# Last pair of heads: splits of the output weights held behind scaled k, the projection's shares in another order, and the second feed-forward's first weights laid off the residual

## The chip, the cores and the metric

The kernel runs on one core of one Trainium2 chip. The metric is the device time of one execution in microseconds (us). Before the change it was 1968.99 us, the median of three runs (1968.15 to 1970.13).

## What is computed

One layer of a macaron block on x of 1024 rows by 1024 columns, in float32: a half-weighted SwiGLU feed-forward (inner width 2816), stick-breaking attention with 16 heads of 64, and a second half-weighted SwiGLU feed-forward. Each part has an RMS norm in front of it and is added to the residual x.

```
x = x + 0.5 * swiglu(rms_norm(x, n1), wi1, wo1)
xn = rms_norm(x, mix_norm)
q, k, v = heads(xn @ w_qkv);  q, k = rms_norm(q, q_gain), rms_norm(k, k_gain)
z = q @ k^T / 8
w[t, s] = sigmoid(z[t, s]) * prod over s < j < t of (1 - sigmoid(z[t, j])),  for s < t
x = x + concat_heads(w @ v) @ w_o
x = x + 0.5 * swiglu(rms_norm(x, n2), wi2, wo2)
```

## The kernel before

**Numbers in two parts.** A matmul operand is kept as a high part (`fp32r`, written by ACT in `split`, L179) and a low part (operand minus high part, written by POOL or DVE, L180). `mm3` (L271 to L273) multiplies high by high, low by high and high by low, three matmuls for each step of the contraction.

**Stages.** The first feed-forward and the second one work by seven half-size products each. Between them stand the attention and its output projection. The rows t lie in two halves of 512, each in blocks `tb` of 128; `ORDER` names the blocks as 4, 5, 6, 7, 0, 1, 2, 3.

**Attention.** The heads are taken in eight pairs p. One pair has four parts a, b, c, d (`PARTS`, 61 units of time together), one for each head and half of the rows. Every step of the attention is put into `plan` with a time in these units, and the steps are recorded in the order of their times (L970): the scores of a block (`scores`, L817 to L830: matmul, two sigmoids on ACT, a scan on DVE, a product on POOL), the turn of the weights on PE and their split (`turn`, L852), the product with v (`apply`, L870), the q, k, v of the next pair (`qkv`), and the scaled and turned q and k (`prep_q`, `prep_k`, L775 to L780). At the end of q, k, v of a half, POOL writes scaled k into `qk` (L755, L758). Each engine works off its own list in order, so a step that waits holds up what stands behind it on that engine.

**Output of a pair.** For pairs 0 to 6 the result o is split and stored to the scratch tensors `o_keeph` and `o_keepl` (L884) by SP's DMA queue; `load_o` (L895) reads them back into `xh` and `xl`, half 1 of the rows in the seventh pair and half 0 in the eighth. The eighth pair's o is split straight into `xh` and `xl` (L886).

**Projection.** w_o is taken in two halves of its columns. For the first half `out_weights` (L984) loads two k-blocks at a time into `raw0` or `raw1` in turn (512 KB, L987) and splits them; there are four such loads, wo0 to wo3, and the third and fourth reuse the buffers of the first and second. `ON_POOL` says whose low part goes to POOL (all four; DVE's otherwise), `WO_FIRST` into which tiles the parts go. `project(tb, ks, 0)` adds the product of row block tb over the pairs ks to the residual half `x0` (DVE, L1000). `SHARES` gives the times within the last pair at which the eight blocks get their sum over k = 0 to 6, so that this work fills PE beside the last pair's attention; the eight products with k = 7, which need the last pair's o, follow after it. Then come the second half's weights and products (k = 0 to 7, into `x1`), with the norm of finished blocks beside them.

**Places in memory.** The pools of `PROJECTION` lie in one stretch of SBUF in the order of the list, and the second feed-forward's tiles are laid over the same stretch later: a tile of the later stage waits for the last reader of what lay there. `first_weights` (L335) splits the first eight units of w2_in into the tiles u0 to u7, before the stream of further weights begins; `first_pair` (L344) multiplies with them: for the first 256 columns of rows all four products, and in front of the fourth `turn_rest`, the last transposes of the normed rows.

**What sets the order.** Every instruction gets a rank when it is recorded; what is recorded `as_at(mark)` gets the rank of that mark. A scheduler then fills each engine's list by rank and by when its own model has the operands ready, so work of a late rank can be moved ahead into a gap of the model. The marks of the shares come from the plan; w_o's first loads and splits have `marks[0]` (d 15.5 of the seventh pair), and stand earlier than that in the lists.

Of the kernel before, what the change touches and what calls it, by code (L numbers as in the profile page):

```python
# [9 lines left out]
F32 = mybir.dt.float32  # L10
# [3 lines left out]
ALU = mybir.AluOpType  # L14
# [3 lines left out]
P = 128  # L18
# [8 lines left out]
NP = H // 2  # L27
# [3 lines left out]
ORDER = (4, 5, 6, 7, 0, 1, 2, 3)  # L31

BANKS = {"bz": 3, "bq": 2, "bt": 2, "bo": 1, "ka": 2, "kc": 2, "kb": 4, "ma": 4, "mb": 4}

ON_POOL = {"wo0", "wo1", "wo2", "wo3"}

# [6 lines left out]

LOADS = (("c", 14.0), ("c", 15.0), ("d", 9.0), ("d", 10.0))

SHARES = (("b", 6.0), ("b", 11.0), ("c", 3.0), ("c", 9.0), ("c", 15.0), ("d", 1.5), ("d", 5.0), ("d", 8.5))

TURN, APPLY = 4.0, 2.3  # L50
RAW = 6
# [2 lines left out]
U_TILES = 18  # L54
# [35 lines left out]
    6: ((0, 1), (0, 0), "subtract"), 7: ((1, 0), (1, 1), "subtract"),  # L90
}

SHARE = 7


PROJECTION = ("wa", "x0", "wb", "wc", "we", "wf", "wg", "wd", "wh", "wi", "wj", "wk", "wl", "x1")
WO_FIRST = ("raw2", "raw3", "raw4", "raw5", "wa", "wb", "wd", "wc")
WO_SECOND = ("we", "wf", "wg", "wh", "wi", "wj", "wk", "wl")
EARLY = ("bq",)
ROUND = ("bq", "bt", "bq", "bt", "bo")  # L100
# [3 lines left out]
def macaron_kernel(ctx, tc, x, g1, w1_in, w1_out, gm, w_qkv, gq, gk, w_o, g2, w2_in, w2_out, out):  # L104
# [8 lines left out]
    def lane(name):  # L113

        return pool_e if name in ON_POOL else dve

# [52 lines left out]
    make_identity(nc, ident)  # L169
    xh = cpool.tile([P, KD, T], F32R, name="xh")  # L170
    xl = cpool.tile([P, KD, T], F32R, name="xl")
    above = cpool.tile([P, 112], F32, name="above")
    pool_e.memset(below, 0.0)
    pool_e.memset(above, 0.0)
    x_keep = [dram.tile([T, D], F32, name=f"x_keep{i}") for i in range(2)]
# [2 lines left out]
    def split(raw, hi, lo, engine=None):  # L178
        act.activation(hi, raw, AF.Copy)  # L179
        (engine or dve).tensor_tensor(lo, raw, hi.bitcast(F32), op=ALU.subtract)  # L180
# [151 lines left out]

    T0, T1 = HALVES[1], HALVES[0]

    def first_weights(pl, raws, behind=None):  # L335

        place["u"] = place["h"] = 0
        return {
            (j, part): [unit(pl, columns(raws[part][d], j), pool_e, behind) for d in range(2)]
            for part in range(2)  # L340
            for j in range(2)
        }

    def first_pair(pl, us, turns):  # L344

        hb = {}
        n = 0  # L350
        for t, c in ((0, T0), (1, T1)):
            ps = {key: bank("ka" if key[1] == 0 else "kc") for key in us}
            for c0 in range(0, NHALF, CHUNK):
                cc = slice(c.start + c0, c.start + c0 + CHUNK)
                for i, (key, w) in enumerate(us.items()):
                    if (n, i) in turns:
                        turns[n, i]()
                    mm3(
                        ps[key][:, c0 : c0 + CHUNK],
                        [  # L360
                            ((w[k // 4][0][:, k % 4], w[k // 4][1][:, k % 4]), (xh[:, k, cc], xl[:, k, cc]))
                            for k in range(KD)
                        ],
                    )
                n += 1
            for j in range(2):
                h = small(pl, "h")
                g = pl[f"h{place['h'] + 3}"].tile([P, NHALF], F32, name="h", bufs=1)
                act.activation(g, ps[j, 0], AF.Silu)
                dve.tensor_tensor(h, ps[j, 1], g, op=ALU.mult)  # L370
                hb[j, t] = h
        return hb
# [299 lines left out]
    on_banks = ExitStack()  # L672
    on_banks.enter_context(banks("psa"))

    marks = []
    with ExitStack() as stack:
        pl = dict(stack.enter_context(pools(
# [247 lines left out]
        for p in range(-1, NP):  # L925
            this = states[p] if p >= 0 else None
            nxt = states[p + 1] if p < NP - 1 else None
            start, t = {}, PAIR * p
            for part, span in PARTS.items():
                start[part], t = t, t + span  # L930

            def put(part, t, f):
                plan.append((start[part] + t, f))

            for part, span in PARTS.items():
                state = nxt if part == "d" else this
                if state is not None:
                    spread(scores(state, *UNITS[part]), start[part], start[part] + span, 0.5)
                if this is not None:
                    groups = values(this, p, *BEFORE[part])  # L940
                    for i, (to_turn, to_apply) in enumerate(groups):
                        t = TURN + (span - TURN) * i / len(groups)
                        put(part, t, to_turn)
                        put(part, t + APPLY, to_apply)
            if nxt is not None:
                if p >= 0:
                    fills = qkv(p + 1, nxt)
                    for part, span in PARTS.items():
                        for i in range(FILLS[part]):
                            put(part, (span - (3.0 if part == "d" else 0.0)) * (i + 0.5) / FILLS[part], fills.pop(0))  # L950
                put("c", 15.0, partial(prep_q, nxt, 1))
                put("c", 17.5 if p >= 0 else 20.0, partial(prep_k, nxt, 0, 1))
                put("d", 8.0, partial(prep_k, nxt, 1, 1))
            if this is not None:
                put("a", 5.0, partial(prep_q, this, 0))
                put("a", 7.5, partial(prep_k, this, 0, 0))
                put("b", 8.0, partial(prep_k, this, 1, 0))
            if 0 <= p < NP - 2:

                held = (lambda s=nxt: s["qk", 1][:, 0, 4, 0:1], lambda s=nxt: s["qk", 0][:, 2, 0, 0:1])  # L960
                for at, f in zip(LOADS, weights_of(p + 2, states[p + 2], held)):
                    put(*at, f)
            if p == NP - 2:
                put("c", 10.0, partial(load_o, 1))
                put("d", 15.5, lambda: marks.append(tc.cur_priority))
            if p == NP - 1:
                put("a", 2.5, partial(load_o, 0))
                for at in SHARES:
                    put(*at, lambda: marks.append(tc.cur_priority))
        for _, f in sorted(plan, key=lambda e: e[0]):  # L970
            f()
# [8 lines left out]
    with pools(*PROJECTION) as pl:  # L980
        pl = pl | pr | pn
        x_sb = [pl[f"x{h}"].tile([P, NT, NHALF], F32, name=f"x{h}", bufs=1) for h in range(2)]

        def out_weights(c, k, rooms):  # L984

            raw = pl[f"raw{k // 2 % 2}"].tile([P, D], F32, name="raw", bufs=1)
            sp.dma_start(  # L987
                raw.rearrange("p (k c) -> p k c", k=2),
                w_o[k * P : (k + 2) * P, c].rearrange("(k p) c -> p k c", p=P),
            )  # L990
            h_, l_ = (pl[n].tile([P, D], F32R, name=n.rstrip("2345"), bufs=1) for n in rooms[k : k + 2])
            split(raw, h_, l_, lane(f"wo{k // 2}") if c is HALVES[0] else dve)
            return [(h_[:, s], l_[:, s]) for s in HALVES]

        def project(tb, ks, h, tags):

            o = any_bank(tags)
            t = rows(tb)
            mm3(o, [((xh[:, k, t], xl[:, k, t]), wo[k]) for k in ks])
            dve.tensor_tensor(x_sb[h][:, tb, :], o, x_sb[h][:, tb, :], op=ALU.add)  # L1000

        wo = []
        place["raw"] = 2
        for k in range(0, NP, 2):
            with as_at(marks[0]):
                wo += out_weights(HALVES[0], k, WO_FIRST)
        with as_at(marks[0]):
            for tb in ORDER:
                sp.dma_start(x_sb[0][:, tb, :], x_keep[0][rows(tb), HALVES[0]])
        for i, tb in enumerate(ORDER):  # L1010
            with as_at(marks[1 + i]):
                project(tb, range(SHARE), 0, EARLY)
        for tb in ORDER:
            sp.dma_start(x_sb[1][:, tb, :], x_keep[0][rows(tb), HALVES[1]])
        gain = load_gain(pl, g2)
        for tb in ORDER:
            project(tb, range(SHARE, NP), 0, ROUND)
        wo = []
        for k in range(0, NP, 2):
            wo += out_weights(HALVES[1], k, WO_SECOND)  # L1020
        ahead = [stream(pr, w2_in, 0, part) for part in range(2)]
        for i, tb in enumerate(ORDER):
            project(tb, range(NP), 1, ("bt",))
            for bk in ("bz", "bz" if i == 6 else "bq")[: len(pending)]:
                pending.pop(0)(bk, tl)
            for h, c in enumerate(HALVES):
                sp.dma_start(x_keep[1][rows(tb), c], x_sb[h][:, tb, :])
            if i % 2:
                pending.extend(norm(pl, lambda tb, h: x_sb[h][:, tb, :], ORDER[i - 1 : i + 1], gain))
# [6 lines left out]

    ops = {}
    with banks("ps3"), pools(*STREAM) as pa:
        hb = first_pair(pa | pr, first_weights(pa | pr, ahead), {(0, 3): turn_rest})
        with pools(*SPLIT) as pt:  # L1040
            ffn_in(pa | pr | pt, w2_in, keep, tl, hb, right, lambda: early(pr, w2_out, keep, ops))
    with banks("ps4"), pools(*SECOND) as pl:
# [55 lines left out]
```

## Time and profile before

| what | value |
|---|---|
| median of three runs | 1968.99 us (1968.15 to 1970.13) |
| the profiled execution | 1967.96 us, of it 1966.2 us span |
| mean granted clock of TensorE | 0.997 |
| PE busy | 1917.2 us, 98% of the span |
| PE weight loads busy | 1641.7 us, 83% |
| DVE, ACT, POOL busy | 1248.8 us (64%), 983.4 us (50%), 1086.9 us (55%) |

The span is the stretch from the first to the last instruction; 1.76 us of the profiled execution lie around it. PE is the matmul engine; its weight loads run beside its matmuls. A row of the timeline gives the start and the duration of an instruction (or of several alike), and in brackets how long its engine had been idle and what ended that.

### The profile page before, as it was taken

The numbers are of one execution on the slowest core, as the hardware profiler recorded it, in microseconds if no ns is written. First come the engines' busy times: TensorE is split into PE (matmuls) and PEld (weight loads), VectorE is DVE, ScalarE is ACT, GpSimd is POOL, SyncE is SP. The second block draws the span as 40 slices with busy tenths as digits, with TensorE's granted clock in tenths as the row PEclk, the third lists the DMA queues.
The fourth block names the chain that finished last, engine by engine and source line by source line (L and its number), as shares of the span: only waits on it lengthen the run. The fifth ranks groups of instructions, "written<-read, shape, count | busy, mean of one in ns | idle before, by whom it ended". The sixth has DMA issues, their size and how long they took to land.

```text
span 1966.2 us, 27322 instructions
## 1 busy us (share of the span) xinstructions
PE 1917.2 (98%) x9656; PEld 1641.7 (83%) x9656; DVE 1248.8 (64%) x1823; ACT 983.4 (50%) x1802; POOL 1086.9 (55%) x957
## 2 busy tenths in 40 slices
PE   7999999999999899999999999999999999999999
PEld 7978888888888798898889897789888888888887
DVE  7855545536767667877787778474645644547644
ACT  6533433443335467777777776344343343343332
POOL 3667666656445445555655645113666666755454
PEclk9999999999999999999999999999999999999999
DMA  5223323238996311111111234411332332359984
GB/s 209 86 93 122 106 88 120 95 123 287 355 321 222 105 33 44 38 39 44 36 37 42 66 103 164 166 60 54 118 102 100 121 102 86 124 195 350 317 274 148
DMA packets 168504, 260.25 MB, mean 132 GB/s; under 512 B 11568, under 2 KB 81200, under 8 KB 168368
## 3 DMA queue, kind: packets, MB, share of 16 engines
q1 hardware_dynamic: 168368, 258.52, 38.3%
q8 instruction: 75, 1.23, 0.3%
q14 instruction: 61, 0.50, 0.1%
HBM read 198.18 MB, written 60.29 MB: 131 GB/s over the span
## 4 chain that ended last, share of the span: by engine, by line
PE 79%; DVE 9%; POOL 4%; ACT 4%; issue 3%; DMA 1%; SPq 0%; ACTq 0%; DVEq 0%; POOLq 0%
PE ka L271 6%; PE ka L272 6%; PE ka L273 6%; PE kc L273 4%; PE kc L272 4%; PE kc L271 4%; PE kb L272 4%; PE kb L273 4%; PE kb L271 4%; PE bq L271 3%; PE bq L272 3%; PE bq L273 3%; PE ma L271 3%; PE ma L272 3%; PE ma L273 3%
## 5 line engine op out<-in xcount | busy, mean ns | idle before, releaser
L180 POOL TENSOR_TENSOR rp<-raw,rp 128x1024 fp32r<-128x1024 f32 x84 | 205.8, 2453 | 189.7 <-ACT rp L179 174.5
L180 POOL TENSOR_TENSOR u<-sf,u 128x512 fp32r<-128x512 f32 x160 | 225.9, 1413 | 152.3 <-ACT u L179 148.4
L180 POOL TENSOR_TENSOR u<-raw,u 128x512 fp32r<-128x512 f32 x136 | 195.8, 1445 | 173.4 <-ACT u L179 172.4
L830 POOL TENSOR_TENSOR w<-w,om 128x512 f32<-128x512 f32 (+4 forms) x128 | 142.4, 1115 | 120.0 <-DVE om L823 93.6
L179 ACT ACTIVATE u<-sf 128x512 fp32r<-128x512 f32 x160 | 100.7, 630 | 215.3 <-PE kb L272 86.8
L390 DVE TENSOR_TENSOR h<-h 128x512 f32<-128x512 f32 x110 | 135.3, 1235 | 88.6 <-POOL h L494 87.9
L271 PE MATMUL bq<-wqh,xh 128*128 128x384 f32 x512 | 174.6, 341 | 2.1 <-DVE vst L744 2.1
L179 ACT ACTIVATE rp<-rh 128x1024 fp32r<-128x1024 f32 (+1 forms) x78 | 76.5, 984 | 198.4 <-issue 65.4
L273 PE MATMUL bq<-wqh,xl 128*128 128x384 f32 x512 | 172.2, 336 | 0.0
L272 PE MATMUL bq<-wql,xh 128*128 128x384 f32 x512 | 172.1, 336 | 0.0
L271 PE MATMUL ka<-xh,u 128*128 128x512 f32 (+1 forms) x448 | 162.2, 362 | 1.9 <-ACT s L442 1.4
L179 ACT ACTIVATE u<-raw 128x512 fp32r<-128x512 f32 x136 | 85.0, 632 | 154.9 <-PE ka L272 101.3
L272 PE MATMUL ka<-xl,u 128*128 128x512 f32 (+1 forms) x448 | 161.9, 361 | 0.0
L273 PE MATMUL ka<-xh,u 128*128 128x512 f32 (+1 forms) x448 | 161.6, 361 | 0.0
L515 DVE TENSOR_TENSOR raw<-raw 128x1024 f32<-128x1024 f32 (+1 forms) x60 | 86.4, 1445 | 96.4 <-DMA raw<-w_out 76.4
L273 PE MATMUL ma<-rp 128*128 128x512 f32 x352 | 137.6, 391 | 3.6 <-DVE rp L180 3.6
L271 PE MATMUL ma<-rp 128*128 128x512 f32 x352 | 137.9, 392 | 0.1
L272 PE MATMUL ma<-rp 128*128 128x512 f32 x352 | 137.6, 391 | 0.0
L821 ACT ACTIVATE w<-bz,f 128x512 f32<-128x512 f32 (+1 forms) x192 | 112.8, 587 | 46.2 <-PE bz L817 40.6
L494 POOL TENSOR_TENSOR h<-h,g 128x512 f32<-128x512 f32 x80 | 112.5, 1406 | 32.7 <-DVE h L446 32.7
L419 DVE TENSOR_TENSOR sf<-raw 128x512 f32<-128x512 f32 x80 | 80.2, 1003 | 78.0 <-POOL u L180 78.0
L180 DVE TENSOR_TENSOR rp<-rh,rp 128x1024 fp32r<-128x1024 f32 (+1 forms) x70 | 110.0, 1590 | 19.2 <-ACT rp L179 16.7
(253 smaller groups left out, 5550.1 us busy)
## 6 DMA issues: line engine op xcount, KB each, us to landing
raw<-w_out SPq DMA_DIRECT2D x120, 512.0 KB, 5.7
raw<-w_in SPq DMA_DIRECT2D x88, 512.0 KB, 3.5
k<-h SPq DMA_DIRECT2D x154, 256.0 KB, 2.1
rh<-k SPq DMA_DIRECT2D x64, 512.0 KB, 6.0
raw_qkv<-w_qkv SPq DMA_DIRECT2D x64, 192.0 KB, 2.9
x_keep<-x SPq DMA_DIRECT2D x32, 256.0 KB, 2.9
x<-x_keep SPq DMA_DIRECT2D x32, 256.0 KB, 5.0
raw<-w_out SPq DMA_DIRECT2D x24, 256.0 KB, 4.2
```

The source lines that it names most:

```text
L179: act.activation(hi, raw, AF.Copy)
L180: (engine or dve).tensor_tensor(lo, raw, hi.bitcast(F32), op=ALU.subtract)
L271: pe.matmul(dst, ah, bh, start=start and i == 0, stop=False, skip_group_check=onto)
L272: pe.matmul(dst, ah, bl, start=False, stop=False, skip_group_check=onto)
L273: pe.matmul(dst, al, bh, start=False, stop=stop and i == n - 1, skip_group_check=onto)
L390: dve.tensor_tensor(src, hb[of[0]], hb[of[1]], op=getattr(ALU, of[2]))
L419: dve.tensor_tensor(f[n], x, y, op=op)
L494: pool_e.tensor_tensor(h, h, gs[k], op=ALU.mult)
L515: dve.tensor_tensor(w[0], w[0], w[1], op=getattr(ALU, W_OF[m][2]))
L821: act.activation(to, z, AF.Sigmoid, scale=state["f", half][:, sign, tb % 4, hd : hd + 1])
L830: pool_e.tensor_tensor(wt[:, c1 : c0 + n], wt[:, c1 : c0 + n], om[:, c1 - 1 : c0 + n - 1], op=ALU.mult)
```

## The change

1. `ON_POOL` loses wo3: the low part of the fourth w_o load is DVE's.
2. In the plan of the seventh pair two steps `note` are added. Each is a POOL product of one element per partition that reads scaled k of the last pair (half 1's `qk`) or its turned low part (`kl_s` of the first head, half 1) into a new tile `seen`. In `out_weights`, for wo0 and wo1, a POOL product of one element writes the low part's tile from `seen` before the split does.
3. `PROJECTION` and `WO_FIRST` are laid out anew: wa, wb, wc now lie in front of x0, and the parts of wo2 are wa and wd, those of wo3 wb and wc.
4. `SHARES` now names times, blocks and ranges of k. Blocks 4, 5, 0, 1 get k = 0 to 6, blocks 6 and 7 the whole sum, blocks 2 and 3 k = 0 to 6, then blocks 4 and 5 their k = 7; after the last pair only the k = 7 of blocks 0 to 3 is left. There are 14 additions to x0 on DVE where there were 16.
5. `first_weights` starts at the tile u16: its eight units are u16, u17, u0 to u5.

```diff
-ON_POOL = {"wo0", "wo1", "wo2", "wo3"}
+ON_POOL = {"wo0", "wo1", "wo2"}
-SHARES = (("b", 6.0), ("b", 11.0), ("c", 3.0), ("c", 9.0), ("c", 15.0), ("d", 1.5), ("d", 5.0), ("d", 8.5))
+SHARES = (
+    (("b", 6.0), 4, (0, 7)), (("b", 11.0), 5, (0, 7)), (("c", 3.0), 0, (0, 7)), (("c", 9.0), 1, (0, 7)),
+    (("c", 15.0), 6, (0, 8)), (("d", 1.5), 7, (0, 8)), (("d", 5.0), 2, (0, 7)), (("d", 8.5), 3, (0, 7)),
+    (("d", 10.5), 4, (7, 8)), (("d", 12.5), 5, (7, 8)),
+)
-PROJECTION = ("wa", "x0", "wb", "wc", "we", "wf", "wg", "wd", "wh", "wi", "wj", "wk", "wl", "x1")
-WO_FIRST = ("raw2", "raw3", "raw4", "raw5", "wa", "wb", "wd", "wc")
+PROJECTION = ("wa", "wb", "wc", "x0", "we", "wf", "wg", "wd", "wh", "wi", "wj", "wk", "wl", "x1")
+WO_FIRST = ("raw2", "raw3", "raw4", "raw5", "wa", "wd", "wb", "wc")
...
-    def first_weights(pl, raws, behind=None):
+    def first_weights(pl, raws, behind=None, at=0):
-        place["u"] = place["h"] = 0
+        place["u"], place["h"] = at, 0
...
+    seen = cpool.tile([P, 2], F32, name="seen")
...
             if p == NP - 2:
+                def note(i, f):
+                    pool_e.tensor_tensor(seen[:, i : i + 1], f(), f(), op=ALU.mult)
+                put("c", 14.0, partial(note, 0, lambda s=nxt: s["qk", 1][:, 0, 4, 0:1]))
+                put("d", 1.0, partial(note, 1, lambda s=nxt: s["k", 0, 1][1][:, 0:1].bitcast(F32)))
...
             h_, l_ = (pl[n].tile([P, D], F32R, name=n.rstrip("2345"), bufs=1) for n in rooms[k : k + 2])
+            if c is HALVES[0] and k < 4:
+                there = seen[:, k // 2 : k // 2 + 1]
+                pool_e.tensor_tensor(l_[:, 0:1], there, there, op=ALU.mult)
             split(raw, h_, l_, lane(f"wo{k // 2}") if c is HALVES[0] else dve)
...
-        for i, tb in enumerate(ORDER):
+        for i, (_, tb, pairs) in enumerate(SHARES):
             with as_at(marks[1 + i]):
-                project(tb, range(SHARE), 0, EARLY)
+                project(tb, range(*pairs), 0, EARLY)
...
-        for tb in ORDER:
-            project(tb, range(SHARE, NP), 0, ROUND)
+        for tb in ORDER[4:]:
+            project(tb, range(NP - 1, NP), 0, ROUND)
...
-        hb = first_pair(pa | pr, first_weights(pa | pr, ahead), {(0, 3): turn_rest})
+        hb = first_pair(pa | pr, first_weights(pa | pr, ahead, at=U_TILES - 2), {(0, 3): turn_rest})
```

A program that lists what each engine works off shows what this moves. Line numbers of the changed kernel are 3 to 13 higher.

POOL before, at the end of the sixth pair, where `qk` of the seventh pair's half 0 is scaled (L755, L758) and the first two w_o loads are split (`raw<-raw`, 128x1024):

```order
L828 MEMSET w_11752 128x1
L830 TENSOR_TENSOR w_11752<-w_11752 128x127
L180 TENSOR_TENSOR raw<-raw 128x1024
L828 MEMSET w_11784 128x1
L828 MEMSET w_11806 128x1
L830 TENSOR_TENSOR w_11784<-w_11784 128x511
L755 TENSOR_TENSOR qk_11352<-qk_11352,r 128x4x128
L180 TENSOR_TENSOR raw<-raw 128x1024
L758 TENSOR_TENSOR qk_11352<-qk_11352,r 128x4x64
L830 TENSOR_TENSOR w_11806<-w_11806 128x383
L758 TENSOR_TENSOR qk_11352<-qk_11352,r 128x4x64
```

POOL with the change, in the middle of the seventh pair, where `qk` of the last pair's half 1 is scaled (now L759, L762):

```order
L759 TENSOR_TENSOR qk_11795<-qk_11795,r 128x4x128
L762 TENSOR_TENSOR qk_11795<-qk_11795,r 128x4x64
L832 MEMSET w_12260 128x1
L970 TENSOR_TENSOR seen<-qk_11795 128x1
L762 TENSOR_TENSOR qk_11795<-qk_11795,r 128x4x64
L1004 TENSOR_TENSOR raw<-seen 128x1
L183 TENSOR_TENSOR raw<-raw 128x1024
L834 TENSOR_TENSOR w_12260<-w_12260,om 128x255
L834 TENSOR_TENSOR w_12260<-w_12260,om 128x512
L832 MEMSET w_12332 128x1
L834 TENSOR_TENSOR w_12332<-w_12332,om 128x127
```

The split of wo0 has moved from the first place to the second, and that of wo1 too, to just behind the last row shown, after its own two one-element products. SP's third load of w_o, which takes the buffer of wo0, has moved with it: in SP's list it stood right ahead of a pair of `o_keeph` and `o_keepl` stores (the third of three loads in a row), and now it stands with the fourth behind `load_o`'s reads of half 1.

ACT before, also in the middle of the seventh pair, around the high part of the last pair's turned k for half 1 (`kh_s`):

```order
L179 ACTIVATE th<-bt 128x384
L821 ACTIVATE w_12330<-bz,f_11739 128x128
L821 ACTIVATE bz<-bz,f_11739 128x128
L779 ACTIVATE q_s_12317<-bz,gq_sb 64x512
L779 ACTIVATE kh_s_12349<-bz,gk_sb 128x512
L179 ACTIVATE th<-bt 128x512
L821 ACTIVATE w_12330<-bz,f_11739 128x512
```

ACT with the change:

```order
L825 ACTIVATE w_12332<-bz,f_11740 128x128
L825 ACTIVATE bz<-bz,f_11740 128x128
L783 ACTIVATE q_s_12319<-bz,gq_sb 64x512
L182 ACTIVATE wa<-raw 128x1024
L783 ACTIVATE kh_s_12351<-bz,gk_sb 128x512
L182 ACTIVATE th<-bt 128x512
L825 ACTIVATE w_12332<-bz,f_11740 128x512
```

The high part of wo2 (`wa<-raw`) stood 58 rows ahead of `kh_s` before; now it stands right ahead of it, behind the turned q.

POOL before, at the end of the projection, with buffer numbers: the low parts of the second feed-forward's first eight units (u_14054 and on in steps of 4, in the order of their use by PE), one unit of the stream behind (u_14589), and two sums of the norm (tl3):

```order
L180 TENSOR_TENSOR u_14070<-raw_13503,u_14069 128x512
L180 TENSOR_TENSOR u_14062<-raw_13499,u_14061 128x512
L180 TENSOR_TENSOR u_14054<-raw_13499,u_14053 128x512
L180 TENSOR_TENSOR u_14058<-raw_13501,u_14057 128x512
L262 TENSOR_TENSOR tl3_13098<-tl3_13098,tl1_13096 128x4x128
L180 TENSOR_TENSOR u_14066<-raw_13501,u_14065 128x512
L180 TENSOR_TENSOR u_14589<-raw_14584,u_14588 128x512
L262 TENSOR_TENSOR tl3_13098<-tl3_13098,tl1_13096 128x4x128
L180 TENSOR_TENSOR u_14074<-raw_13505,u_14073 128x512
L180 TENSOR_TENSOR u_14078<-raw_13503,u_14077 128x512
L180 TENSOR_TENSOR u_14082<-raw_13505,u_14081 128x512
```

POOL with the change, where the first eight are u_14055 and on in steps of 4:

```order
L183 TENSOR_TENSOR u_14067<-raw_13502,u_14066 128x512
L183 TENSOR_TENSOR u_14075<-raw_13506,u_14074 128x512
L183 TENSOR_TENSOR u_14083<-raw_13506,u_14082 128x512
L183 TENSOR_TENSOR u_14079<-raw_13504,u_14078 128x512
L183 TENSOR_TENSOR u_14059<-raw_13502,u_14058 128x512
L183 TENSOR_TENSOR u_14063<-raw_13500,u_14062 128x512
L265 TENSOR_TENSOR tl3_13101<-tl3_13101,tl1_13099 128x4x128
L183 TENSOR_TENSOR u_14071<-raw_13504,u_14070 128x512
L183 TENSOR_TENSOR u_14055<-raw_13500,u_14054 128x512
L265 TENSOR_TENSOR tl3_13101<-tl3_13101,tl1_13099 128x4x128
L183 TENSOR_TENSOR u_14590<-raw_14585,u_14589 128x512
```

Before, the two units used first (u_14054, u_14058) were the third and fourth of the eight, and the last three were the sixth to the eighth in the order of use. Now the unit used first (u_14055) comes last of the eight, behind the low parts of the other seven and one sum of the norm.

## Rows read from the trace of the kernel before

**Rows 1.** Timeline (start, us, engine, line): PE and ACT, 1128 to 1130 us.
```profile
1129.94 0.39 PE L817 MATMUL bz<-kh_s,q_s 128*128 128x256 f32 x1 [2.05 <-DVE w L823]
...
1128.35 0.47 ACT L821 ACTIVATE w<-bz,f 128x256 f32<-128x256 f32 x1 [2.35 <-DMA o_keeph<-w]
```
**Rows 2.** Timeline of SP, 1112 to 1132 us: three loads of w_o.
```profile
1115.18 8.01 SPq L987 DMA_DIRECT2D raw<-w_o  x3
```
**Rows 3.** The two stores of line L884 issued from 1123 to 1125 us.
```profile
DMA to landing us min/median/max: 5.0/5.5/5.9
```
**Rows 4.** The two stores of line L884 issued from 1079 to 1082 us.
```profile
DMA to landing us min/median/max: 2.0/2.0/2.0
```
**Rows 5.** Timeline of POOL, 1118 to 1130 and 1159 to 1174 us.
```profile
1126.35 2.37 POOL L180 TENSOR_TENSOR raw<-raw 128x1024 fp32r<-128x1024 f32 x1
...
1162.60 0.62 POOL L758 TENSOR_TENSOR qk<-qk,r 128x256 f32<-128x256 f32 x1
```
**Rows 6.** The two single loads of w_o (L987) issued from 1200 to 1240 us.
```profile
DMA to landing us min/median/max: 3.6/3.8/3.9
```
**Rows 7.** Timeline: ACT (1132 and 1167 us), DVE and PE (1168 to 1170 us).
```profile
1132.31 1.08 ACT L179 ACTIVATE wa<-raw 128x1024 fp32r<-128x1024 f32 x1
...
1167.22 0.69 ACT L779 ACTIVATE kh_s<-bz,gk_sb 128x512 fp32r<-128x512 f32 x1 [0.55 <-PE bz L775]
...
1168.70 0.69 DVE L180 TENSOR_TENSOR tl<-bt,th 128x512 fp32r<-128x512 f32 x1
...
1169.46 0.37 PE L870 MATMUL bo<-tl,vst 128*128 128x256 f32 x1
```
**Rows 8.** Timeline of POOL, PE and DVE, 1184 to 1190 us.
```profile
1184.41 2.39 POOL L180 TENSOR_TENSOR wb<-raw,wa 128x1024 fp32r<-128x1024 f32 x1
...
1189.62 0.33 PE L852 MATMUL bt<-ident,w 128*128 128x128 f32 x1 [1.84 <-POOL w L828]
...
1187.91 1.23 DVE L823 TENSOR_TENSOR_SCAN w<-bz,first 128x512 f32<-128x512 f32 x1 [0.31 <-ACT bz L821]
```
**Rows 9.** Two stretches: length, busy PE, PEld, DVE, ACT, POOL; PEclk; DMA.
```profile
1120.00:1140.00 20.00, 17.46 (x102) 14.99 (x100) 14.45 (x26) 16.68 (x34) 13.65 (x17) 1.00 0.27 80
...
1180.00:1200.00 20.00, 18.16 (x102) 15.62 (x101) 15.34 (x35) 13.38 (x30) 11.49 (x16) 0.91 0.88 296
```
**Rows 10.** Timeline of DVE (1183, 1265, 1270 us) and POOL (1270 us).
```profile
1182.95 0.69 DVE L823 TENSOR_TENSOR_SCAN w<-bz,first 128x256 f32<-128x256 f32 x1 [1.18 <-ACT bz L821]
...
1264.95 1.21 DVE L180 TENSOR_TENSOR wj<-raw,wi 128x1024 fp32r<-128x1024 f32 x1
...
1269.97 2.06 DVE L180 TENSOR_TENSOR wl<-raw,wk 128x1024 fp32r<-128x1024 f32 x1
...
1269.66 1.29 POOL L180 TENSOR_TENSOR u<-raw,u 128x512 fp32r<-128x512 f32 x1 [6.64 <-ACT u L179]
```
**Rows 11.** Timeline of PE and ACT, 1264 to 1266 us.
```profile
1264.37 0.50 PE L271 MATMUL bo<-wd,xh 128*128 128x512 f32 x1 [0.82 <-DVE o L876]
1264.70 0.39 PE L272 MATMUL bo<-wc,xh 128*128 128x512 f32 x1
1264.93 0.40 PE L273 MATMUL bo<-wd,xl 128*128 128x512 f32 x1
1265.86 0.50 PE L271 MATMUL bt<-wd,xh 128*128 128x512 f32 x1 [0.52 <-ACT xh L179]
...
1264.24 1.05 ACT L179 ACTIVATE wk<-raw 128x1024 fp32r<-128x1024 f32 x1
```
**Rows 12.** Waits of PE from 1300 to 1340 us: in total, times, longest.
```profile
PE kc L271 <- ACT u L179: 2.3, 1, 2.3
PE kc L273 <- POOL u L180: 0.8, 1, 0.8
```
**Rows 13.** Timeline of POOL and PE, 1315 to 1323 us.
```profile
1315.91 2.56 POOL L180 TENSOR_TENSOR u<-raw,u 128x512 fp32r<-128x512 f32 x2 [44.96 <-ACT u L179]
...
1318.66 0.28 PE L273 MATMUL ka<-xh,u 128*128 128x256 f32 x1
```

More of the change, by code (lines that the diff above doesn't have):

```diff
@@ L91 @@
 }
-SHARE = 7
-PROJECTION = ("wa", "x0", "wb", "wc", "we", "wf", "wg", "wd", "wh", "wi", "wj", "wk", "wl", "x1")
-WO_FIRST = ("raw2", "raw3", "raw4", "raw5", "wa", "wb", "wd", "wc")
+PROJECTION = ("wa", "wb", "wc", "x0", "we", "wf", "wg", "wd", "wh", "wi", "wj", "wk", "wl", "x1")
+WO_FIRST = ("raw2", "raw3", "raw4", "raw5", "wa", "wd", "wb", "wc")
 WO_SECOND = ("we", "wf", "wg", "wh", "wi", "wj", "wk", "wl")
@@ L171, in macaron_kernel @@
     xl = cpool.tile([P, KD, T], F32R, name="xl")
-    above = cpool.tile([P, 112], F32, name="above")
+    above = cpool.tile([P, 104], F32, name="above")
     pool_e.memset(below, 0.0)
@@ L967, in macaron_kernel @@
                 put("a", 2.5, partial(load_o, 0))
-                for at in SHARES:
+                for at, _, _ in SHARES:
                     put(*at, lambda: marks.append(tc.cur_priority))
```

## The prediction

> **What bounds the kernel now.** PE is busy for 98% of the span, so time comes or goes only where PE stands idle, where its clock is halved, or where matmuls are added; the change adds none. I read the waits of PE first, from 1100 to 1340 us, where every edited line runs, and then the timelines around each wait. The reader should see four idle places. A: 2.05 us at 1129.94 behind a scan [rows 1]. C: 1.84 us at 1189.62 behind POOL [rows 8]. F: 0.82 and 0.52 us around the last pair's result [rows 11]. G: 2.3 and 0.8 us at the second feed-forward's first weights [rows 12]. Then the stretches with their clock [rows 9]: the one with C has a mean granted clock of 0.91, so TensorE ran part of it at 1.2 instead of 2.4 GHz, and (1 − 0.91) × 20 = 1.8 us of matmul time were lost behind C. The stretch with A stayed at 1.00. So the clock is a possible second charge for a wait, not a sure one.
>
> The sum is made against the profiled execution (1967.96 us). The median of the runs is 1968.99, 1.03 us above it; I add that at the end.
>
> **The change, part by part.**
>
> *A goes: −2.05.* Scan and matmul wait at A for ACT's sigmoid, and that for the store of o_keeph, which had to land before its tile was overwritten (2.35 us idle) [rows 1]. The two stores took 5.0 and 5.9 us to land [rows 3]; the same stores one pair earlier took 2.0 [rows 4]. What stood ahead of them were three loads of w_o of 512 KB, the third issued just before them, at the end of 1115.18 + 8.01 [rows 2]. The change sends that load away to the middle of the seventh pair. A store that lands 3 us sooner covers ACT's 2.35 whole. Bounds: −2.05, and 0 should the store stay slow for another reason.
>
> *A new stall on ACT: +3.1.* The third load waits for POOL to finish wo0's split. POOL ends its scaled k at 1162.60 + 0.62; two one-element products stand around it, which no row here prices (between nothing and the 0.62 of 256 columns each; I take 0.15 each, near the lower end for one column), then the split of 2.37 [rows 5]: 1165.9. A lone load of w_o lands 3.6 to 3.9 us after its issue [rows 6], so the data is there at 1169.5 at the earliest. ACT's list now has wo2's high part, which needs that load, right ahead of kh_s. Before, kh_s began at 1167.22 [rows 7]. Now ACT stands until 1169.5, spends 1.08 on wa (0.95 until the next may follow), and kh_s starts at about 1170.4: 3.2 late. Behind it stand th, then DVE's tl, which ended at 1169.39, and PE's apply began with it at 1169.46 [rows 7], no slack. So PE stands about 3.1 us, less the 0.07. Bounds: 0, if ACT were late there anyhow, and +4.2, if the load takes a microsecond more. I take 3.1, since every link has a row. Price by the skill: the Trainium skill (DMA: Bandwidth & Descriptors, "Anatomy of one DMA — SWDGE (gpsimd) path") fits 2.0 us plus the bytes at 436 GB/s, 3.2 us for 512 KB, an estimate, by which the stall would be 2.7; rows 6 show 3.6 and more here.
>
> *The clock behind that stall: +1.8.* An idle time of 3.1 us is longer than C, which was followed by half clock. Bounds 0 (as behind A) and 1.8. I take 1.8, since 3.1 lies beyond both.
>
> *C goes: −2.8.* At C, POOL was on wo2's and wo3's low parts, 2.39 us the first and the second right behind, ahead of the product that PE waited for [rows 8]. Now wo3's is DVE's and wo2's stands earlier on POOL, where it waits less. The 1.84 goes, and 1.8 of clock. Given back: the scan that PE's next scores need ends at 1187.91 + 1.23 = 1189.14 [rows 8], 0.5 before PE resumed, with the matmuls behind it late likewise; I take 0.8. Bounds −3.6 (nothing late) and −1.0 (the clock falls all the same).
>
> *wo3's low part on DVE: +0.4.* DVE's split of 128x1024 takes 1.21 us when POOL is idle, 2.06 when POOL works beside it [rows 10]. It comes right ahead of a scan with 1.18 us of idle time in front [rows 10]: 0 to 0.9 over; I take 0.4, for half an overlap. The Trainium skill (GPSIMD Engine Reference, "Specifications") says that POOL shares its SBUF interfaces with VectorE, with contention when a DVE instruction has two SBUF inputs. The two durations agree, and by that rule 0.9 would be due here.
>
> *Notes and touches:* four one-element products on POOL, counted above where they delay the load; the second pair stands beside POOL's idle time (55% busy), and if that cover went, it would cost the same 0.3 us again. *Two x0 additions fewer* are DVE time beside PE's work: 0.
>
> *F: +1.4.* Before, the twelve k = 7 matmuls of the first four of eight blocks filled PE's wait for the last result, 0.23 us each [rows 11], 2.8 us. Now they come earlier, into stretches where PE was full, and the wait is bare. In return xh's high part stands ahead of wk on ACT, which frees it by about 1.05 us [rows 11], and POOL and DVE have fewer additions between. 2.8 − 1.05 − 0.35 (of the old idle 0.82 + 0.52, the part that the earlier xh takes away besides) = 1.4. Bounds +0.9 and +2.2, the latter if the second half's first product waits for DVE's wl split, 2.06 [rows 10].
>
> *G: +0.5.* The units laid off the residual no longer wait for the norm, so 2.3 + 0.8 = 3.1 goes. But the unit that PE uses first is now the last of the eight on POOL. POOL began at 1315.91, with two splits in 2.56 [rows 13]. Five such steps, four splits and a sum of the norm as long, end at 1322.3, and PE's third matmul wanted that low part at 1318.66 [rows 13]: a wait of 3.6. Bounds −3.1 (the low part is in time) and +1.0.
>
> Sum: −2.05 + 3.1 + 1.8 − 2.8 + 0.4 + 1.4 + 0.5 = +2.35; 1967.96 + 2.35 = 1970.3, and on the median's footing 1971.3. A measurement of this kernel can tell 0.2%, 3.9 us, from no change (1965.1 to 1972.9), so this counts as the same.
>
> **The rivals.**
>
> 1. *The clock holds behind ACT's stall.* For it: A, 2.05 us long, left 1.00 [rows 9]. Against: C. 1971.3 − 1.8 = 1969.5.
> 2. *No stall on ACT.* The load lands before ACT comes to it, or the whole stretch is later by other waits. For it: A and C shift POOL and ACT against each other. Against: no link in the chain has slack. Both terms go: 1971.3 − 4.9 = 1966.4. If A, C and the tail then also come out at their better bounds (−0.8 at C, −0.4 on DVE, −0.5 at F), 1964.7, faster.
> 3. *The residual part does what it says.* The first unit's low part is in time, because POOL is ahead of its old hours: G is −3.1 instead of +0.5, 1971.3 − 3.6 = 1967.7; together with rival 1, 1965.9, with rival 2, 1962.8. Against: ACT's high part of that unit is itself bound to the second half's matmuls.
> 4. *Slower: the bare tail halves the clock.* PE now stands in several pieces between the last apply and xh, with about 2.4 us for the chain o, o, xh alone. If TensorE drops to 1.2 GHz there as after C, add 1.8, and 0.8 with it for the wait on wl: 1971.3 + 2.6 = 1973.9. It decides at about C's length, 1.84.
>
> **How the numbers follow.** Forecast 0.37, rival 1 0.13, rival 2 0.15, rival 3 0.10, rival 4 0.25. The likeliest is the forecast, 1971.3, by itself 1968 to 1974. The low end of the range is rival 2 with its better bounds, rounded to 1965; the high end is rival 4 with the upper bound of ACT's stall, 1973.9 + 1.1, and a microsecond of the tail's: 1976. Slower: rival 4 for the most part (0.20) and a share of the forecast (0.08), 0.28. Faster: half of rivals 2 and 3 and a little of rival 1, 0.2. Same: the rest, 0.52.
>
> **What would show it.** Right: no wait of PE at the old A and C; ACT idle before wa, released by DMA, for some 2.9 us, and PE idle some 3 us at the apply behind it; a stretch of half clock after that; two or three waits of PE in the tail before xh; a wait of about 3.6 us at the third matmul on the first weights, released by POOL. Wrong: ACT's wa without idle time before it, the first weights without a wait, or a wait of PE over 1 us at a place not named here.

## The result, and the profile of the changed kernel

The changed kernel takes 1975.39 us (median of 12 runs, 1973.28 to 1980.71), the kernel before, run beside it, 1970.00 (12 runs, 1967.95 to 1975.36). The ratio is 1.0031, 95% interval 1.0020 to 1.0041: slower by about 6 us, 4 to 8. The forecast was a sum of +2.35 us, which it called no change.

The profiled execution of the changed kernel is the longest of its twelve, 1980.71 us; part of its excess over the kernel before is missing in the shorter ones, as shown below.

Waits of PE from 1120 to 1345 us in the changed kernel (in total, times, longest):

```profile
PE ka L276 <- POOL u L183: 3.4, 1, 3.4
PE bo L874 <- ACT th L182: 2.9, 2, 2.5
...
PE bt L274 <- ACT xh L182: 2.3, 1, 2.3
```

A and C are gone, and three new waits stand in their place. Where time came and went is read best from the start of one and the same matmul in both traces. At 1110 us the changed kernel's are 1.2 us late, from the program's start, the first feed-forward and the earlier pairs of heads, which the change doesn't touch. From there on the lateness grows by (a row with a minus: shrinks by):

| place | shift in the trace, us | forecast, us |
|---|---|---|
| A, the store of o_keeph (1120 to 1134) | −2.5 | −2.05 |
| ACT's stall and the clock behind it (1168 to 1175) | +4.7 | +3.1 + 1.8 |
| C and wo3's low part on DVE (1186 to 1202) | −1.8 | −2.8 + 0.4 |
| F, the tail of the last pair (1237 to 1270) | +3.2 | +1.4 |
| G, the first weights (1318 to 1334) | −0.2 | +0.5 |
| sum so far | +3.4 | +2.35 |
| second feed-forward, 1757 us | +1.8 | 0 |
| second feed-forward, 1950 us | +6.4 | 0 |

1.2 + 3.4 + 1.8 + 6.4 is the 12.8 us by which this execution exceeds the profiled one of before. The shortest runs of the two kernels differ by 1973.28 − 1967.95 = 5.3, about 3.4 + 1.8, and six of the twelve lie within 1.3 us of the shortest: so the last row is not in every execution of the changed kernel. In how many it is, isn't known: only this one was profiled.

**A and the stall.** The two stores landed thus (line L888, issued from 1122 to 1126 us), where they had taken 5.0 and 5.9 [rows 3]:

```profile
DMA to landing us min/median/max: 2.5/2.9/3.3
```

The third and fourth load of w_o, ACT and PE behind them (timelines):

```profile
1164.64 9.78 SPq L997 DMA_DIRECT2D raw<-w_o  x2
...
1168.46 1.06 ACT L182 ACTIVATE wa<-raw 128x1024 fp32r<-128x1024 f32 x1 [3.05 <-DMA raw<-w_o]
1169.55 0.69 ACT L783 ACTIVATE kh_s<-bz,gk_sb 128x512 fp32r<-128x512 f32 x1
...
1170.77 0.50 PE L874 MATMUL bo<-th,vst 128*128 128x256 f32 x1 [2.54 <-ACT th L182]
1171.67 0.58 PE L874 MATMUL bo<-tl,vst 128*128 128x256 f32 x1 [0.40 <-DVE tl L183]
```

The chain is the one forecast, link by link: the load is issued as POOL's split ends, ACT waits 3.05 us (2.9 was forecast), and PE 2.54 + 0.40. The two loads landed in 3.6 and 3.8 us. The estimate of 3.2 us worked out from the Trainium skill (DMA: Bandwidth & Descriptors, "Anatomy of one DMA — SWDGE (gpsimd) path") was short here by 0.4 and more; the section's fit is for transfers on the gpsimd path, and these loads are issued by SP.

**Clock.** Stretches of the changed kernel (length, busy PE, PEld, DVE, ACT, POOL, then PEclk and DMA), the second to be held against [rows 9]:

```profile
1160.00:1180.00 20.00, 17.07 (x99) 15.74 (x98) 11.45 (x20) 12.16 (x26) 12.24 (x17) 0.91 0.17 54
1180.00:1200.00 20.00, 19.18 (x118) 16.48 (x117) 17.36 (x37) 15.16 (x32) 9.71 (x15) 1.00 0.86 282
1260.00:1280.00 20.00, 17.05 (x72) 13.35 (x71) 10.38 (x15) 7.86 (x14) 5.10 (x4) 0.91 0.80 261
1320.00:1340.00 20.00, 16.57 (x115) 15.78 (x115) 13.23 (x27) 6.41 (x14) 8.77 (x7) 0.91 0.32 93
1750.00:1770.00 20.00, 18.07 (x80) 14.66 (x79) 12.24 (x12) 7.53 (x9) 11.34 (x6) 1.00 0.75 242
1940.00:1960.00 20.00, 16.69 (x62) 13.21 (x61) 12.48 (x13) 4.46 (x5) 11.54 (x6) 0.83 0.35 127
```

The first, third and fourth of these stretches in the kernel before:

```profile
1160.00:1180.00 20.00, 20.00 (x126) 18.58 (x125) 15.29 (x25) 14.90 (x33) 9.36 (x14) 1.00 0.10 30
...
1260.00:1280.00 20.00, 18.65 (x85) 14.78 (x84) 11.72 (x17) 7.04 (x13) 2.58 (x2) 1.00 0.64 225
...
1320.00:1340.00 20.00, 16.84 (x126) 16.43 (x125) 14.35 (x27) 7.73 (x14) 9.22 (x8) 0.91 0.31 94
```

The clock fell behind the stall and no longer falls at C. At the first weights it fell before (0.91) and falls with the change (0.91), behind other waits. It also fell behind the tail, which rival 4 had and the forecast had not:

```profile
1265.43 0.38 PE L874 MATMUL bo<-th,vst 128*128 128x256 f32 x1 [0.33 <-ACT th L182]
1266.16 0.39 PE L874 MATMUL bo<-tl,vst 128*128 128x256 f32 x1 [0.34 <-DVE tl L183]
...
1269.06 0.50 PE L274 MATMUL bt<-wb,xh 128*128 128x512 f32 x1 [2.28 <-ACT xh L182]
```

The bare wait is there in three pieces, 2.95 us, where it was 0.82 + 0.52 [rows 11].

**The first weights.** POOL and PE, to be held against [rows 13]:

```profile
1320.69 2.55 POOL L183 TENSOR_TENSOR u<-raw,u 128x512 fp32r<-128x512 f32 x2 [43.98 <-ACT u L182]
1323.20 1.27 POOL L265 TENSOR_TENSOR tl<-tl,tl 128x512 f32<-128x512 f32 x1
1324.43 2.49 POOL L183 TENSOR_TENSOR u<-raw,u 128x512 fp32r<-128x512 f32 x2
...
1326.98 0.39 PE L276 MATMUL ka<-xh,u 128*128 128x256 f32 x1 [3.40 <-POOL u L183]
```

The low part that PE uses first is the second of the later two, behind three splits and a sum, and PE waits 3.40 us (3.6 was forecast).

**Outside the stretch that I looked at.** At 1757 us, in the second feed-forward, no wait stood before. Now PE waits for a product h (L449) of DVE, which stands behind an addition in DVE's list:

```profile
1754.92 1.28 POOL L497 TENSOR_TENSOR h<-h,g 128x512 f32<-128x512 f32 x1 [1.82 <-PE ka L276]
1756.16 2.38 POOL L183 TENSOR_TENSOR rp<-raw,rp 128x1024 fp32r<-128x1024 f32 x1
...
1756.24 2.86 DVE L393 TENSOR_TENSOR h<-h 128x512 f32<-128x512 f32 x1 [1.45 <-POOL h L497]
1759.02 0.68 DVE L449 TENSOR_TENSOR h<-ka,s 128x512 f32<-128x512 f32 x1
...
1759.75 0.50 PE L274 MATMUL ma<-rp 128*128 128x512 f32 x1 [1.93 <-DVE h L449]
```

DVE's addition takes 2.86 us beside POOL's split, and the product that PE waits for comes behind it. And at 1950 us:

```profile
1953.53 0.79 PE L276 MATMUL ma<-rp 128*128 128x512 f32 x1 [3.31 <-DVE rp L183]
```

### The profile page after: what moved, and what is told of

It is laid out like the page before. It is cut to its first block, busy times and chain, and to the rows that moved or that the text cites. A ratio compares the mean times of both kernels' runs of the same rounds, so it can differ in the third digit from the quotient of the medians.

```text
span 1978.9 us, 27327 instructions
## 1 busy us (share of the span) xinstructions
PE 1922.6 (97%) x9656; PEld 1645.1 (83%) x9656; DVE 1259.5 (64%) x1822; ACT 985.4 (50%) x1802; POOL 1085.3 (55%) x960
## 3 DMA queue, kind: packets, MB, share of 16 engines
q8 instruction: 75, 1.23, 0.3%
## 5 line engine op out<-in xcount | busy, mean ns | idle before, releaser
L518 DVE TENSOR_TENSOR raw<-raw 128x1024 f32<-128x1024 f32 (+1 forms) x60 | 103.1, 1720 | 90.7 <-DMA raw<-w_out 82.2
L182 ACT ACTIVATE th<-bt 128x512 fp32r<-128x512 f32 (+1 forms) x160 | 93.1, 586 | 50.5 <-PE bt L856 28.2
```

What stands on the lines that cost most here:

```text
L518: dve.tensor_tensor(w[0], w[0], w[1], op=getattr(ALU, W_OF[m][2]))
```

## The experiments

Theory 1, after the result: the loss is made of ACT's stall (+4.7), the tail (+3.2) and a wait of 1.8 that the turned ring of u tiles causes at 1757 us, against gains at A and C. Theory 2: the excess is the late wait near 1950 us, which the change makes likelier. Each experiment was timed beside the kernel before; a ratio is to that, with its 95% interval, and the changed kernel's is 1.0031.

**The ring started at u0 again.**

```diff
-first_weights(pa | pr, ahead, at=U_TILES - 2)
+first_weights(pa | pr, ahead, at=0)
```

> The changed kernel with the second feed-forward's first units back at u0 to u5 and so on (only the start of the ring of 18 tiles is undone). Theory 1 (three places cost: ACT's stall with half clock +4.7 us, the bare tail with half clock +3.2, and 1.8 at a wait of PE near 1757 us that the turned ring causes through another order on POOL and ACT; gains are A -2.5 and C -1.8): no PE wait near 1757 us, the waits at the first weights back to about 2.3 and 0.8, time 1.5 to 2.1 us under the changed kernel, that is about 3.5 us over the kernel before. Theory 2 (the excess is the late wait near 1950 us, which the change makes likelier by its stores and loads): the wait near 1757 may go or stay, the time within 1 us of the changed kernel.

Measured: 1968.12 us (12 runs), ratio 0.9997 (0.9987 to 1.0006). That is 0.0034, some 6.7 us, under the changed kernel, more than three times what was expected. POOL and DVE at the same place as above, some 4 us earlier:

```profile
1745.01 5.74 POOL L183 TENSOR_TENSOR rp<-raw,rp 128x1024 fp32r<-128x1024 f32 x2
1750.70 1.30 POOL L497 TENSOR_TENSOR h<-h,g 128x512 f32<-128x512 f32 x1
...
1752.03 0.69 DVE L393 TENSOR_TENSOR h<-h 128x512 f32<-128x512 f32 x1 [2.95 <-POOL h L497]
1752.64 0.68 DVE L449 TENSOR_TENSOR h<-ka,s 128x512 f32<-128x512 f32 x1
```

Both splits now stand ahead of the products, the addition takes 0.69, and the wait is gone: so the ring's start alone makes it. PE's list is the same in the two kernels; ACT, POOL and DVE differ by a few swapped rows, most of them hundreds of us behind the edit, since the start turns the places of all later units too. The larger part was not expected: PE has no wait from 1300 to 1345 us at all. The places in memory explain it. A unit takes two tiles, one for each part, so the first eight units take sixteen: u0 to u15 when the ring starts at u0, and u16, u17, u0 to u13 when it starts at u16 (not the eight tiles that the text on the kernel and the change names). Counted along the two lists of pools, u10 to u15, the sixth to eighth unit, lay on the residual x0 before. With the new places u8 to u13 lie on wa, wb and wc, which hold weights of the first half, and u14, u15 on x0; u16, u17 lie on wi, which the last product of the second half reads behind wf, wg and wh, where u0 to u7 lie but for u4 and u5. So with the ring from u0 only the eighth unit waits for the norm, and PE uses it behind `turn_rest`. ACT's list shows it, before and in this run, each time behind the norm's xs:

```profile
1327.42 1.67 ACT L179 ACTIVATE u<-raw 128x512 fp32r<-128x512 f32 x3 [7.14 <-DVE xs L234]
...
1332.79 0.64 ACT L182 ACTIVATE u<-raw 128x512 fp32r<-128x512 f32 x1 [7.12 <-DVE xs L237]
```

With the ring from u16 the eighth unit leaves x0 too, but the unit used first lies on wi. The shift at the first weights is −5.3 against before, where the changed kernel has −0.2: the waits of 2.3 and 0.8 go, and the half clock behind them with them (mean clock from 1320 to 1340 us 1.00 here, 0.91 before).

**The high part of wo2 held as well.**

```diff
+            if c is HALVES[0] and k == 4:
+                there = seen[:, 1:2]
+                pool_e.tensor_tensor(h_[:, 0:1], there, there, op=ALU.mult)
             split(raw, h_, l_, lane(f"wo{k // 2}") if c is HALVES[0] else dve)
```

> The changed kernel with one more one-element product: the high part of wo2 is also held, behind the turned low part of k, so that ACT takes it eight rows later, behind kh_s and the apply's result. Theory 1: no DMA wait of ACT ahead of kh_s, no PE wait of 2.5 us near 1168 us and no half clock at 1171 to 1174; time 4 to 4.7 us under the changed kernel, about 1 us over the kernel before. Rival (the wait only moves: ACT meets the same load eight rows later, or POOL's wait at C with its half clock returns because all arrive sooner): at most 2 us gained, with a new PE wait between 1170 and 1200 us.

Measured: 1970.36 us (12 runs), ratio 1.0009 (1.0000 to 1.0019), 0.0022 or 4.3 us under the changed kernel. ACT:

```profile
1164.63 0.69 ACT L783 ACTIVATE kh_s<-bz,gk_sb 128x512 fp32r<-128x512 f32 x1 [0.58 <-PE bz L779]
...
1168.47 1.05 ACT L182 ACTIVATE wa<-raw 128x1024 fp32r<-128x1024 f32 x1
```

wa starts when it did in the changed kernel's trace, without idle time ahead of it, and kh_s 4.9 us earlier, of which 1.3 are a lead that this execution had already at 1167 us. PE has no wait over 0.6 us from 1150 to 1200, so the wait did not move.

**The shares of before.**

```diff
-    (("c", 15.0), 6, (0, 8)), (("d", 1.5), 7, (0, 8)), (("d", 5.0), 2, (0, 7)), (("d", 8.5), 3, (0, 7)),
-    (("d", 10.5), 4, (7, 8)), (("d", 12.5), 5, (7, 8)),
...
-        for tb in ORDER[4:]:
+        for tb in ORDER:
```

> The changed kernel with the shares of before: blocks in the order 4, 5, 6, 7, 0, 1, 2, 3 with k = 0 to 6, and all eight k = 7 products after the last pair. Theory 1: the 2.3 us wait of PE ahead of the last k = 7 products shrinks to about 0.8 and 0.5 with no half clock behind it, time 2.5 to 3.2 us under the changed kernel, about 2.5 us over the kernel before. Theory 2, or if the early k = 7 products fill other idle time: less than 1 us gained.

Measured: 1976.86 us (6 runs, 1973.29 to 1978.65), ratio 1.0035 (1.0021 to 1.0048): no gain, as theory 2 had it. The profiled execution was the shortest, 1973.29, and there the tail did give back what was expected: its shift is +0.6 instead of +3.2, PE's waits these:

```profile
PE bo L275 <- DVE o L881: 1.5, 1, 1.5
PE bt L275 <- ACT xh L183: 0.5, 1, 0.5
```

But the wait at 1757 us brought half clock with it, which it had not in the changed kernel's profile (mean clock of the stretch 1.00):

```profile
1750.00:1770.00 20.00, 18.05 (x73) 14.43 (x72) 13.83 (x13) 6.77 (x9) 11.72 (x7) 0.91 0.74 244
```

3.4 us instead of 1.8. What made four of the other five runs 3.4 to 5.4 us longer than this one no profile shows. So the run left the price of the tail open, and it was taken again below, without the turned ring.

**All three together.** The hold of wo2's high part, the shares of before, the ring from u0.

> All three undone or mended together: high part of wo2 held, shares of before, ring started at u0; kept are the hold of the splits behind scaled k, the fourth low part on DVE and the new places. Theory 1: gains A and C are left, time about 4.3 us under the kernel before (range 2.5 to 5). Rival (the gains at A and C depend on the stall that follows): within 1.5 us of the kernel before.

Measured: 1959.38 us (6 runs, 1958.44 to 1964.36), ratio 0.9956 (0.9942 to 0.9970): 8.7 us under the kernel before, twice what was expected; its trace has the 5.3 at the first weights, which the expectation left out. PE's waits from 1120 to 1345 us:

```profile
PE bt L857 <- POOL w L835: 1.7, 3, 1.2
PE bo L875 <- DVE tl L184: 1.7, 3, 1.2
PE bo L275 <- DVE o L881: 0.8, 1, 0.8
```

Nothing above 1.2 us is left, nor any wait after 1345, nor half clock after the first feed-forward until the last matmul. This version beats both kernels.

**wo3's low part back on POOL**, in that version.

```diff
-ON_POOL = {"wo0", "wo1", "wo2"}
+ON_POOL = {"wo0", "wo1", "wo2", "wo3"}
```

> The mended version (e4_late_shares_at0) with the low part of the fourth load of w_o back on POOL. If the wait at C was POOL having two splits in a row, it returns: PE idle 1.5 to 2.4 us at a turn near 1187 us, with or without half clock behind it, time 1.5 to 3.5 us over e4_late_shares_at0. Rival (it is enough that the third load's low part stands earlier): within 1 us of e4_late_shares_at0.

Measured: 1959.36 us (6 runs), ratio 0.9953 (0.9938 to 0.9969). No difference beyond the noise, the rival was right; C does not return. POOL:

```profile
1177.34 2.40 POOL L184 TENSOR_TENSOR wd<-raw,wa 128x1024 fp32r<-128x1024 f32 x1
1179.83 2.39 POOL L184 TENSOR_TENSOR wc<-raw,wb 128x1024 fp32r<-128x1024 f32 x1
...
1182.22 0.74 POOL L835 TENSOR_TENSOR w<-w 128x255 f32<-128x255 f32 x1
```

The two splits still stand in a row, but they now run ahead of the 255-column product, in time in which POOL was idle; before, they stood behind it [rows 8]. The trace has one wait of PE that the mended version's has not, with what ACT waited for in front of it:

```profile
1195.87 0.47 PE L822 MATMUL bz<-kh_s,q_s 128*128 128x512 f32 x1 [0.99 <-DVE w L828]
...
1194.19 0.47 ACT L826 ACTIVATE w<-bz,f 128x256 f32<-128x256 f32 x1 [1.76 <-DMA o_keeph<-w]
```

Through C the shift is −0.6 in this trace and −1.8 in the mended version's. Whether POOL's fourth split or a store that happened to land late makes this wait isn't shown.

**The shares of the change**, in the mended version.

> The mended version with the changed kernel's shares (the early k = 7 products and the bare tail) and nothing else undone. If the tail costs what the traces' shift shows: PE idle about 2.3 us ahead of the last k = 7 products, time 2.2 to 2.8 us over e4_late_shares_at0 without half clock behind it, 4 to 4.5 with it. Rival (the run with the shares of before was no faster than the changed kernel, so the tail costs nothing): within 1 us of e4_late_shares_at0.

Measured: 1963.72 us (8 runs), ratio 0.9969 (0.9959 to 0.9980). Beside the 0.9953 of the experiment above, which was timed on the same chip and differs in wo3's low part too, that is 3 us dearer by the ratios and 4.4 by the medians; beside the mended version itself it is 2.6 and 4.3. PE's wait in the tail:

```profile
PE bt L274 <- ACT xh L182: 2.3, 1, 2.3
```

And the stretch with it:

```profile
1260.00:1280.00 20.00, 16.84 (x62) 13.34 (x62) 7.62 (x10) 6.26 (x12) 3.35 (x3) 0.83 0.58 193
```

So the tail costs, and its clock is the larger part: (1 − 0.83) × 20 = 3.4 us of a shift of 4.7 in this execution.

**The places alone**, in the kernel before.

```diff
-PROJECTION = ("wa", "x0", "wb", "wc", "we", "wf", "wg", "wd", "wh", "wi", "wj", "wk", "wl", "x1")
-WO_FIRST = ("raw2", "raw3", "raw4", "raw5", "wa", "wb", "wd", "wc")
+PROJECTION = ("wa", "wb", "wc", "x0", "we", "wf", "wg", "wd", "wh", "wi", "wj", "wk", "wl", "x1")
+WO_FIRST = ("raw2", "raw3", "raw4", "raw5", "wa", "wd", "wb", "wc")
```

> The kernel before with nothing but the new places (wa, wb, wc ahead of x0, and wo2 in wa and wd, wo3 in wb and wc); first units from u0 on. If the places alone free the first units from the norm: no PE wait at the first weights and no half clock behind it, time 4.5 to 5.5 us under the kernel before. Rival (POOL meets the unit used first too late, as in the changed kernel): a wait of 2.5 to 3.5 us there, within 1 us of the kernel before.

Measured: 1964.70 us (11 runs, 1961.37 to 1968.17), ratio 0.9977 (0.9966 to 0.9988), 4.5 us faster. No wait at the first weights (shift −5.3), and C is gone too (shift −1.8). From 1120 to 1200 us only A stands out:

```profile
PE bz L817 <- DVE w L823: 2.1, 1, 2.1
PE bt L852 <- POOL w L828: 0.6, 1, 0.6
```

The profiled execution (1966.33) also shows a late wait of PE, 3.3 us at 1940, with half clock, worth 5.3. The two shifts together are 7.1 us; the four shortest of the eleven runs (1961.37 to 1962.47) lie 6.0 to 7.1 under the median of the kernel before, 1968.51.

**The hold alone**, of wo0, wo1 and wo2's high part, in the kernel before.

> The kernel before with nothing but the hold of the first two splits behind scaled k and of wo2's high part behind turned k. If the wait at A was the third load of w_o against the store of o_keeph: no PE wait at 1127 to 1130 us, stores landing in 2 to 3 us, and the wait at C as before; time 2 to 2.6 us under the kernel before. Rival (the gain at A is given back at C, where POOL now has more to do): within 1 us of the kernel before.

Measured: 1966.75 us (12 runs), ratio 0.9991 (0.9981 to 1.0001): 1.8 us, a little less than expected, with an interval that just reaches no change. The trace shows A gone (shift −2.4) and C whole:

```profile
PE bt L853 <- POOL w L829: 2.4, 2, 1.8
```

## Why the prediction was wrong

**The step that failed first: "from 1100 to 1340 us, where every edited line runs."** The start of the ring is an edit whose effect doesn't end there. It gives every unit of the second feed-forward another place, and with it another order on three engines; one of the swaps costs a wait at 1757 us, 1.8 us, and 3.4 in the two executions that had half clock behind it. No term, bound or rival stood for it; among the signs of being wrong a wait of over 1 us at an unnamed place was listed, and this is one. Undoing the start alone removes it.

**The term that was mis-sized most: "F: +1.4", measured +3.2.** The bare wait is as described, but the clock fell behind it, as rival 4 had it. I priced half clock at the stall and left it out of the tail, though the wait before xh alone, 2.28 us, is longer than C. That it costs was shown with the mended version, not by undoing it alone.

**C: −2.8 with 0.4 given back, measured −1.8, for a reason that is half wrong.** That wo2's low part stands earlier on POOL was right. But it is the new places that move both splits ahead of the product; they alone remove C, with wo3 still on POOL, and the hold alone leaves it. For wo3's low part on DVE no gain is shown. Of the 3.6 us (wait and clock), 1.8 are given back behind it, not 0.8.

**Right:** A (−2.5 for −2.05), by the cause named (though the stores of 2.0 us that it was measured against are of the other half of the rows, 44 us earlier; those one pair earlier took 2.5 and 2.8); ACT's stall with its clock (+4.7 for +4.9), the 4.3 us that came back when wa was held; the wait at the first weights (3.40 for 3.6). But at the first weights I took the start of the ring for the part that frees the units from the norm, which the places do, and I left out the half clock that stood behind G already. So 5.3 us lay open in the change and were spoiled by one number, the ring's start. Rival 3 had this end, with a chance of 0.1, a gain of 3.1 and another cause, POOL being ahead of its hours.

Put together: −2.5 + 4.7 − 1.8 + 3.2 − 0.2 + 1.8 = +5.2 instead of +2.35, within the 4 to 8 us of the runs. The range held the median, but "no change" did not hold: the tail was 1.8 too small in the sum, the unseen wait adds another 1.8, and the smaller misses (A −0.45, the stall −0.2, C +0.6, G −0.7) nearly cancel. The range's upper end was built from rival 4 and the stall's upper bound, not from the wait at 1757 us: that it held is in part luck.

**Open:** the late wait of 3.3 us at 1940 to 1950 us. It stands in one profile of the changed kernel and in one of the places alone, and in no other; runs some 5 us above their kernel's best occur for the kernel before as well. Where the two begin to differ from the rest can be seen, though. Some 40 us ahead of the wait an addition of DVE (raw, halves of w_out) and a split of POOL meet, in the kernel before thus, and then in the changed kernel:

```profile
1904.23 1.23 DVE L515 TENSOR_TENSOR raw<-raw 128x1024 f32<-128x1024 f32 x1 [13.07 <-POOL rp L180]
...
1904.48 3.25 POOL L180 TENSOR_TENSOR rp<-raw,rp 128x1024 fp32r<-128x1024 f32 x1 [0.27 <-ACT rp L179]
...
1911.15 3.18 DVE L518 TENSOR_TENSOR raw<-raw 128x1024 f32<-128x1024 f32 x1 [13.61 <-DMA raw<-w_out]
...
1910.87 2.39 POOL L183 TENSOR_TENSOR rp<-raw,rp 128x1024 fp32r<-128x1024 f32 x1 [0.27 <-ACT rp L182]
```

In the changed kernel DVE, released by a load, begins 0.28 us behind POOL and takes 3.18 us, and SP then stands 8.15 us at the next loads of w_out, 5.65 before; in the places alone it is 0.11, 3.37 and 8.16. In the eight other profiles DVE begins 0.1 to 0.3 us ahead of POOL and takes 1.22 or 1.23. How this grows into the wait was not followed link by link, and whether the change makes it likelier wasn't settled.

## What to carry to other kernels

Where a ring of buffers is laid over memory that is freed at different times, ask which place the operand used first gets, and follow a turned ring to the end of the program, not to the end of the edit: compare each engine's list there. Before a load is pushed later, look at what stands directly in front of the next chain on the engine that consumes it; a one-element operation that holds the consumer too gave back 4 us. And give every new PE wait as long as those here (1.8 us and more) its chance of half clock in the sum, the same one at each.

## What the runs showed of the hardware

The half clock behind a wait is not decided by the length of the wait alone: 2.05 us at A left the clock at 1.00 [rows 1, 9], 1.84 at C brought it to 0.91; 1.9 us at 1757 did nothing in the changed kernel's profile and cost 1.6 us more in two others' (wo2's high part held as well; the shares of before); the tail's 2.3 us took 0.91 in one and 0.83 in another.

Where DVE and POOL worked side by side, the one that began later paid. DVE's addition of two 128x512 tiles took 0.69 us with POOL idle, and 2.86 where POOL's split had begun 0.08 us ahead of it: its own 0.69 and the 2.30 that the split still ran make 2.99. The Trainium skill (GPSIMD Engine Reference, "Specifications") names that contention for DVE instructions with two SBUF inputs, and the trace agrees; here it lay on PE's path. Of the addition and the split shown under "Open", the first to begin took its usual time in all ten profiles, and the second 0.8 to 2.2 us more: POOL 3.2 to 3.4 instead of 2.4 us in eight, DVE 3.18 and 3.37 instead of 1.23 in two.
